# Transposed attention of a hybrid encoder step: three sets of head pages, gates in slices, values ahead of the last four query tiles, samples beside the last heads

## The chip, the cores and the metric

The kernel runs on one core of one Trainium2 chip. A core has TensorE (PE, the matmuls, with PEld for its weight loads), VectorE (DVE), ScalarE (ACT), GpSimd (POOL) and SyncE (SP, which here only issues DMAs). ACT and POOL issue DMAs as well. Each engine works through its own list of instructions in order. The metric is the device time of one execution in microseconds (us); lower is better.

## What is computed

One inference step of a two-layer encoder. 1168 frames pass through it: 16 meta tokens and 1024 prompt frames of one stream (1040 together, TP in the code) and 8 samples of 16 frames that continue running streams. Each layer has three groups of heads, and this case is about the first, latent attention with 8 heads:

```python
q = (rms_norm(c_q, q_norm) @ w_uq).reshape(B, L, MLA_HEADS, MLA_NOPE + MLA_ROPE)
q_nope, q_rope = q[..., :MLA_NOPE], apply_rope(q[..., MLA_NOPE:], pos)
...
k_nope = jnp.einsum('bkr,rhd->bkhd', c_kv, w_uk)
v = jnp.einsum('bkr,rhd->bkhd', c_kv, w_uv)
...
p = jax.nn.softmax(jnp.where(mask, sc.astype(jnp.float32) * scale, -jnp.inf), axis=-1)
o = jnp.einsum('bhlk,bkhd->blhd', p, v[:, :n_keys])
...
mixed = jnp.concatenate([o_a * jax.nn.silu(z_a), o_m * jax.nn.silu(z_m), o_g * jax.nn.silu(z_g)], axis=-1)
return x + mixed @ w_out, ...
```

The samples do the same attention over 1056 cached latent rows each, in the absorbed form (scores against the latent itself). The other two groups (mLSTM and gated DeltaNet) are through, but for the last of their gates, when the part that is changed begins.

## The kernel before

Data lie in pages, SBUF tiles of 128 partitions by 1200 numbers; there are 28. The program is written by generators ("threads": `gload`, `att_m`, `att`, `samp_load`, `samp_s`, ...) and one main thread (`projs`, then `qkv`, `out_first`, `out_proj`). A planner, `Weave`, runs them against a clock of its own that only matmuls and waits advance: a thread yields a number of us, or the name of something that must be done; when no thread is ready, the main thread gives its next few matmuls as filling. Thus the order of TensorE's matmuls is fixed when the program is built. The framework then places the other engines' instructions, so the lists of ACT and POOL can differ somewhat from the order in the source.

In each layer the attention goes like this. `qkv` makes six query tiles (j of 0 to 5; tiles 0 and 3 hold the rotary part, and two DVE operations and one of POOL a slice write it), stores them to DRAM (`qS`), loads four gated pages of the other groups with `mixload`, makes four key tiles (`kS`), and then the values in nine chunks into six pages (`VV`), among which it splits the four loaded pages into a high and a low part (`mixsplit`, 12 casts on ACT, L437, and 12 subtractions). `gload` loads the queries and keys of one head into a set of four pages and splits them (casts L1523 on ACT, subtractions L1524 on POOL); there are two sets, so head h's load waits until the scores of head h - 2 are all issued (`D1["hd", h - 2]`). `att_m` takes the row maxima of a head (17 or 18 score matmuls and as many reductions L1551), turns them with one transposition (L372), and sends the row through DRAM: ACT stores it (L1559), POOL loads it into partition 112 of `qh` (L383). Only then do the transposed scores of this head in `att` pass: 18 steps a head, in slices of 3, 6 and 9 key blocks; a step is three score matmuls (the first needs no row), an `Exp` on ACT (L1586) and, three steps behind (`LA`), a value product. At the end of a slice DVE takes a reciprocal (L1610) and a product, POOL multiplies by the gate (L1612). The gates of two heads lie in a page `za`, loaded by `gload`, stored by SP after the pair.

`out_first`, the first third of the output projection (96 groups of three matmuls), is the filling beside the heads. The samples follow: `samp_prep`, loads of the cache pages (`latT`, `latN`), `samp_split` (casts L1697 on ACT), scores `samp_s` and products `samp_t`, both of which wait for the end of the attention (`yield "att"`).

## Time and profile before

| | |
|---|---|
| median of 3 runs | 2755.3 us (2754.82 to 2755.98) |
| profiled execution: time | 2752.79 us |
| its span, first to last instruction | 2750.9 us |
| mean granted clock of TensorE | 0.962 |
| end of the projections to end of attention, layer 0 | 843.4 to 1181.9 us |
| the same, layer 1 | 2202.1 to 2536.3 us |

The profiled execution is one more run of the same program. The time of a run is some 2 us longer than the span of its instructions. A clock of 1.00 is TensorE's full speed, 0.50 half of it; a mean between them tells how much of a stretch ran at half speed. A line number names the line of the source; matmuls all stand at L361, in the helper `mm`, and are told apart by their tiles: `pb<-pg,pg` with 96 to 113 rows are scores, `pa<-wk,pg` value products, `pa<-pg,wh` projections.

### The profile page before, as it was taken

How to read it: one execution, taken by the hardware profiler on the slowest of the kernel's cores; microseconds unless marked ns; L12 is line 12 of the kernel's file. 1: busy time of each engine (PE TensorE's matmuls, PEld its weight loads, DVE VectorE, ACT ScalarE, POOL GpSimd, SP SyncE). 2: the span in 40 equal slices, each digit the busy share in tenths (PEclk: the TensorE clock that was granted, in tenths of full speed). 3: DMA queues.
4: the chain of work that ended last, by engine and by line, in shares of the span. 5: the costliest groups of instructions: out<-in, count | busy, mean ns of one | idle time of the engine just before them, and what ended most of it. 6: DMA issues, size and time to landing. Idle time of an engine off the chain costs nothing. (4 is left out here: it accounts for less than half of the span.)

```text
span 2750.9 us, 45261 instructions
## 1 busy us (share of the span) xinstructions
PE 2529.8 (92%) x17310; PEld 2176.9 (79%) x17310; DVE 1533.6 (56%) x3716; ACT 1120.6 (41%) x2635; POOL 753.8 (27%) x857
## 2 busy tenths in 40 slices
PE   6999999999998998789998999999999979987897
PEld 4787888878878886579977878787887878866897
DVE  6677375564352555455565764756544435555736
ACT  5454444544442333343343644444444333333612
POOL 3122222131132423232431231222211333322414
PEclk9999999999999998799999999999999999988898
DMA  3212121121126542264422122212211365312932
GB/s 132 64 41 72 50 71 59 58 67 56 49 88 183 148 118 60 82 193 172 151 79 51 49 65 61 68 49 68 65 49 47 108 184 145 105 51 82 309 114 85
DMA packets 152648, 257.57 MB, mean 94 GB/s; under 512 B 47296, under 2 KB 103216, under 8 KB 152432
## 3 DMA queue, kind: packets, MB, share of 16 engines
q1 hardware_dynamic: 150688, 251.82, 29.6%
q0 software_dynamic: 1472, 2.80, 0.5%
q8 instruction: 137, 2.24, 0.3%
q14 instruction: 79, 0.65, 0.1%
q10 hardware_dynamic: 272, 0.07, 0.0%
HBM read 189.70 MB, written 64.92 MB: 93 GB/s over the span
## 5 line engine op out<-in xcount | busy, mean ns | idle before, releaser
L361 PE MATMUL pa<-pg,wh 128*128 128x384 f32 (+2 forms) x6324 | 1313.6, 352 | 37.6 <-DVE wk L1425 8.4
L361 PEld LDWEIGHTS pa<-pg,wh 128*128 128x128 f32 x6324 | 1111.7, 191 | 76.0 <-DVE wk L1425 9.0
L361 PE MATMUL pb<-pg,pg 128*128 128x128 f32 (+23 forms) x1908 | 446.2, 354 | 62.4 <-DMA pg<-row 34.3
L361 PE MATMUL pa<-pg,wb 128*128 128x384 bf16 (+1 forms) x2208 | 421.4, 330 | 4.7 <-POOL pg L544 3.5
L361 PEld LDWEIGHTS pb<-pg,pg 128*128 128x128 f32 (+7 forms) x1908 | 313.1, 198 | 130.0 <-DMA pg<-row 38.7
L361 PEld LDWEIGHTS <-wb 128*128 128x128 bf16 x2208 | 201.8, 98 | 142.3 <-issue 30.2
L441 POOL TENSOR_TENSOR wh<-wf,wh 128x1024 fp32r<-128x1024 f32 (+1 forms) x61 | 144.5, 2368 | 347.2 <-ACT wh L437 346.8
L361 PE MATMUL pb<-wk,pg 128*128 128x128 f32 (+4 forms) x2168 | 219.9, 248 | 16.6 <-ACT wk L983 5.7
L1586 ACT ACTIVATE wk<-pb 128x320 f32<-128x320 f32 (+8 forms) x288 | 116.0, 407 | 276.9 <-PE pb L361 273.6
L361 PEld LDWEIGHTS pb<-wk,pg 128*128 128x128 f32 (+3 forms) x2168 | 191.2, 160 | 37.9 <-issue 16.5
L361 PE MATMUL pa<-wk,pg 128*128 128x320 f32 (+8 forms) x576 | 200.1, 438 | 1.3 <-DVE wk L1885 1.3
L437 ACT CAST wh<-wf 128x1024 fp32r<-128x1024 f32 (+1 forms) x122 | 126.4, 1036 | 137.9 <-PE pa L361 116.5
L1551 DVE TENSOR_REDUCE sm<-pb 128x1 f32<-128x348 f32 (+9 forms) x232 | 107.6, 491 | 106.5 <-PE pb L361 102.1
L1610 DVE RECIPROCAL wk<-pa 64x320 f32<-64x320 f32 (+2 forms) x48 | 110.6, 2305 | 80.4 <-PE pa L361 78.9
L361 PE MATMUL pb<-wk,wk 32*32 32x16 f32 (+6 forms) x1776 | 110.7, 216 | 15.1 <-DVE wk L1131 5.2
L441 DVE TENSOR_TENSOR wh<-wf,wh 128x1024 fp32r<-128x1024 f32 (+1 forms) x61 | 84.3, 1382 | 63.6 <-ACT wh L437 63.0
L868 DVE SCALAR_TENSOR_TENSOR pg<-pg,vec,pg 128x1192 f32<-128x1192 f32 x72 | 107.3, 1506 | 18.3 <-ACT pg L866 17.9
L1612 POOL TENSOR_TENSOR pg<-wk,pg 64x320 f32<-64x320 f32 (+2 forms) x48 | 43.9, 915 | 252.7 <-DVE pg L1611 244.9
L361 PEld LDWEIGHTS pa<-wk,pg 128*128 128x128 f32 (+1 forms) x576 | 105.2, 205 | 7.4 <-issue 1.4
L457 ACT CAST wb<-wf 128x1024 bf16<-128x1024 f32 x92 | 96.2, 1045 | 26.8 <-PE pa L361 20.1
L693 ACT COPY pg<-pa 128x384 f32<-128x384 f32 (+1 forms) x108 | 52.1, 482 | 132.0 <-PE pa L361 130.8
L361 PEld LDWEIGHTS pb<-wk,wk 32*32 32x32 f32 (+2 forms) x1776 | 73.2, 122 | 33.6 <-issue 9.5
(298 smaller groups left out, 3242.8 us busy)
## 6 DMA issues: line engine op xcount, KB each, us to landing
wf<-win SPq DMA_DIRECT2D x92, 512.0 KB
pg<-latT SPq DMA_DIRECT2D x32, 520.0 KB
pg<-latN SPq DMA_DIRECT2D x32, 512.0 KB
wf<-wout SPq DMA_DIRECT2D x24, 512.0 KB
xa<-wk SPq DMA_DIRECT2D x40, 192.0 KB
mix<-pg SPq DMA_DIRECT2D x12, 584.0 KB
pg<-mix SPq DMA_DIRECT2D x12, 584.0 KB
mix<-pg SPq DMA_DIRECT2D x12, 576.0 KB
```

Of the source, the lines that this page charges most:

```text
L361: W.last = P.matmul(out, lhsT, rhs, start=start, stop=stop)
L437: S.copy(hi, src)
L441: lo_eng.tensor_sub(lo, src, hi.bitcast(F32))
L457: S.copy(wb[:, :n], wf)
L693: S.copy(o[:, s0:s1], ps)
L868: V.scalar_tensor_tensor(y[:, :n], cb[:, j:j + n], vcol(l, "cw", 4 * ti + j), y[:, :n], op0=ALU.mult, op1=ALU.add)
L1551: V.tensor_reduce(mx[:LEN[c], 3 * c + i_:3 * c + i_ + 1], ps[:LEN[c], :n1 - x_], axis=AX.X, op=ALU.min)
L1586: S.activation(pt[:m, :b - a], ps, AF.Exp, scale=-1.0)
L1610: V.reciprocal(rc, po[d, :w])
L1612: G.tensor_mul(z, rc, z)
```

## The change

- Query tiles: only tiles 0 and 1 are made ahead of the keys; the values follow the keys, then the query tiles 2 to 5, then the loads of `mixload` and, after 8 us of the planner's clock, the splits of `mixsplit`. They used to stand among the values. A head's load waits for its query tile (`D1["qt", g]`).
- Head pages: three sets in place of two. Head h's load waits for head h - 3.
- Gates: no `za` pages. Each slice of a head loads its own gate (64 partitions by 320 to 384) into a small tile and stores it from ACT when POOL has multiplied: 24 loads on SP and 24 stores on ACT a layer in place of 4 and 4.
- `att` waits for the values at its first value product, not at its first score.
- Samples: `samp_s` and `samp_t` no longer wait for the end of the attention; `samp_t` takes PSUM tiles only when the attention's accumulator leaves one (`free_pa`).

TensorE's matmuls are the same in number and kind.

```diff
-            gr = 0
-            for j in range(6):
-                if j % 2 == 0:
-                    wh, wl = nxt
-                    nxt = load(j // 2 + 1 if j < 4 else "k")
+
+            def qtile(j, wh, wl):
+                gr = j - 1 - j // 3
                 while not room(1):
                     yield "idle"
...
-                    gr += 1
+                    D1["qt", gr] = 1
                 free(sg)
-            free(*cqh, *cql, *tab)
-            D1["qs"] = 1
-            while not room(2 * (PARTS[0][1] - PARTS[0][0])):
-                yield "idle"
-            A["mx0"] = mixload(*PARTS[0])
+
+            (wh, wl), nxt = nxt, load("k")
+            yield from qtile(0, wh, wl)
+            yield from qtile(1, wh, wl)
             for j in range(4):
                 if j == 0:
-                    wh, wl = nxt
-                    nxt = load("v")
+                    (wh, wl), nxt = nxt, load("v")
...
-            wh, wl = nxt
-            A["w0"] = load("o")
-            sp = mixsplit(A["mx0"])
+            (wh, wl), nxt = nxt, load(1)
...
-                next(sp, None)
-                next(sp, None)
                 yield
-            for _ in sp:
-                pass
             D1["v"] = 1
             free(*ckh, *ckl)
+            for j in (2, 3, 4, 5):
+                if j % 2 == 0:
+                    (wh, wl), nxt = nxt, load(2 if j == 2 else "o")
+                yield from qtile(j, wh, wl)
+            free(*cqh, *cql, *tab)
+            D1["qs"] = 1
+            A["w0"] = nxt
+            while not room(2 * (PARTS[0][1] - PARTS[0][0])):
+                yield "idle"
+            A["mx0"] = mixload(*PARTS[0])
+            t0 = W.t
+            while W.t < t0 + 8000.0:
+                yield "idle"
+            for _ in mixsplit(A["mx0"]):
+                yield "idle"
...
                 yield ("spill", g)
-                if h < 2:
+                yield ("qt", g)
+                if h < 3:
...
-                    yield ("hd", h - 2)
-                    qh, ql, kh, kl = sets[h % 2]
+                    yield ("hd", h - 3)
+                    qh, ql, kh, kl = sets[h % 3]
...
                 D1["grp", h] = W.t / 1000.0
-                if j == 0:
-                    yield from need(1)
-                    A["za", g] = pg()
-                    ld(A["za", g][:, o0:TP], mixS[8 + g][:, o0:TP])
-                    D1["za", g] = 1
...
-            yield "v"
...
+                    if j == 0:
+                        zt[h, s_] = z = wt("Og", 512)[64 * (h % 2):64 * (h % 2) + 64, :b - a]
+                        ld(z, mixS[8 + h // 2][64 * (h % 2):64 * (h % 2) + 64, a:b])
...
-                        if h > 5:
-                            free(*A["sets"][h % 2])
+                        if h > 4:
+                            free(*A["sets"][h % 3])
...
                     if j == 0:
+                        yield "v"
...
-                        if ("za", h // 2) not in D1:
-                            yield ("za", h // 2)
...
-                        rc, z = wt("hp", 528, 3)[r, :w], A["za", h // 2][r, q0:b]
+                        rc, z = wt("hp", 528, 3)[r, :w], zt.pop((h, s_))
                         V.reciprocal(rc, po[d, :w])
                         V.tensor_mul(z, po[r, :w], z)
                         G.tensor_mul(z, rc, z)
                         A["po"] = 0
-                        if s_ == 2 and h % 2:
-                            st(mixS[8 + h // 2][:, o0:TP], A["za", h // 2][:, o0:TP])
-                            free(A["za", h // 2])
+                        S.dma_start(mixS[8 + h // 2][r, q0:b], z)
...
         def samp_s():
-            yield "att"
             for b in range(8):
...
-                    yield 0.00
+                    if "att" in D1:
+                        yield 0.00
...
-                yield from need(1)
                 Pp = pg()
...
+        def free_pa():
+            while A.get("po", 0) and npa[0] - A["po"] > 1:
+                yield 0.2
+
         def samp_t():
-            yield "att"
             for b in range(8):
...
+                    yield from free_pa()
                     ps = pa()
```

What the planner makes of it is seen in three places. The first is TensorE's list at head 4 of layer 0. In the rows `pb<-cst,wk` at L372 is the transposition of the row maxima, `pa<-wk,pg` a value product, and 80x336, 128x256, ... are the score matmuls of a slice. Before:

```order
L361 MATMUL pa_10867<-wk_10916,pg_9499 128x64
L372 MATMUL pb_10937<-cst,wk_10812 128x128
L361 MATMUL pb_10952<-pg_9401,pg_9404 80x336
L361 MATMUL pb_10963<-pg_9584,pg_9582 128x348
L361 MATMUL pb_10966<-pg_9401,pg_9404 128x256
L361 MATMUL pb_10973<-pg_9584,pg_9582 128x348
L361 MATMUL pb_10976<-pg_9401,pg_9404 128x128
L361 MATMUL pb_10988<-pg_9584,pg_9582 128x344
L361 MATMUL pb_10991<-pg_9401,pg_9404 80x384
L361 MATMUL pb_10999<-pg_9584,pg_9582 128x456
L361 MATMUL pb_11002<-pg_9401,pg_9404 128x384
L361 MATMUL pb_10952<-pg_9401,pg_9403 80x336
```

The transposition of head 4's maxima stands between the last value product of head 3 (above it) and head 4's scores: the first of them on `pg_9404` need no row, those on `pg_9403` do, ten rows after the transposition. Now:

```order
L361 MATMUL pb_10646<-pg_9214,pg_9216 128x384
L361 MATMUL pb_10646<-pg_9215,pg_9216 128x384
L361 MATMUL pa_10623<-wk_10596,pg_9308 128x128
L372 MATMUL pb_10658<-cst,wk_10426 128x128
L361 MATMUL pa_10666<-pg_9678,wh_9914 128x384 x2
L361 MATMUL pa_10666<-pg_9679,wh_9914 128x384
L361 MATMUL pb_10674<-pg_9214,pg_9217 128x384
L361 MATMUL pb_10674<-pg_9214,pg_9216 128x384
L361 MATMUL pb_10674<-pg_9215,pg_9216 128x384
```

The same transposition stands amid the scores of head 3 (`pg_9214` to `pg_9217`) and the output projection (`wh_9914`); head 4's first score is the 87th row after it. It is like this for heads 2 to 7 of both layers.

The second place is the start of head 0 in layer 0, on TensorE. Before, the transposition of head 0's maxima, and the output projection behind it:

```order
L372 MATMUL pb_9797<-cst,wk_9594 128x128
L361 MATMUL pa_9810<-pg_9346,wh_9658 128x400 x2
L361 MATMUL pa_9810<-pg_9347,wh_9658 128x400
L361 MATMUL pa_9810<-pg_9348,wh_9658 128x400 x2
L361 MATMUL pa_9810<-pg_9349,wh_9658 128x400
```

Now, from the end of the last query tile (`wh_9445`) on:

```order
L361 MATMUL pa_9658<-pg_9055,wh_9445 128x384
L372 MATMUL pb_9670<-cst,wk_9385 128x128
L361 MATMUL pb_9695<-pg_9375,pg_9373 128x348
L361 MATMUL pb_9698<-pg_9375,pg_9373 128x348
L361 MATMUL pb_9701<-pg_9375,pg_9373 128x344
L361 MATMUL pb_9704<-pg_9375,pg_9373 128x456
L361 MATMUL pb_9709<-pg_9214,pg_9217 80x336
L361 MATMUL pb_9715<-pg_9375,pg_9373 128x456
L361 MATMUL pb_9718<-pg_9214,pg_9217 128x256
L361 MATMUL pb_9724<-pg_9375,pg_9373 128x392
L361 MATMUL pb_9727<-pg_9214,pg_9217 128x128
```

No output projection follows any more; behind the transposition stand row maxima of head 1 (`pg_9375,pg_9373`) and those scores of head 0 that need no row. The first that needs it is the 15th row.

The third place is ACT's list at the change from head 6 to head 7 in layer 0: L1589 is `Exp`, L1697 and L1700 are the casts of the samples' cache pages, and L1616 is the new store of a gate slice. Now:

```order
L1589 ACTIVATE wk_11715<-pb_11711 128x64
L1697 CAST pg_11705<-pg_11696 128x528 x2
L1589 ACTIVATE wk_11736<-pb_11732 80x336
L1589 ACTIVATE wk_11748<-pb_11744 128x256
L1589 ACTIVATE wk_11761<-pb_11757 128x128
L1697 CAST pg_11724<-pg_11699 128x528 x2
L1700 CAST pg_11739<-pg_11702 96x528 x2
L1697 CAST pg_11751<-pg_11718 128x528 x2
L1616 DMA mix<-wk_11580 64x320
L1589 ACTIVATE wk_11775<-pb_11771 80x384
```

Before, the casts of the first cache pages stood beside head 7 as well, but their loads were issued at head 6's start; now the loads are issued near head 6's end. The store L1616 stands one or two `Exp` after the point of the program where it was written.

## Rows read from the trace of the kernel before

**Rows 1.** The profile's page: span and the engines' busy us, share of the span, instructions.
```profile
span 2750.9 us, 45261 instructions
PE 2529.8 (92%) x17310; PEld 2176.9 (79%) x17310; DVE 1533.6 (56%) x3716; ACT 1120.6 (41%) x2635; POOL 753.8 (27%) x857
```

**Rows 2.** Windows, layer 0: length, busy us (count) per engine, clock, DMA share, GB/s.
```profile
843.00:899.00 56.00, 46.12 (x235) 43.82 (x234) 12.45 (x23) 17.98 (x37) 18.27 (x25) 0.91 0.73 212
899.00:937.00 38.00, 33.04 (x157) 29.09 (x156) 23.79 (x41) 11.82 (x26) 20.68 (x23) 0.91 0.55 154
937.00:1050.00 113.00, 110.24 (x594) 96.83 (x594) 66.03 (x97) 38.97 (x90) 32.53 (x35) 0.98 0.38 110
1050.00:1182.00 132.00, 103.91 (x452) 81.08 (x451) 62.30 (x98) 44.57 (x113) 32.47 (x42) 0.79 0.22 61
```

**Rows 3.** Windows, layer 1, the same stages, columns as above.
```profile
2202.00:2258.00 56.00, 44.23 (x224) 42.87 (x224) 10.99 (x20) 16.63 (x34) 16.55 (x21) 0.91 0.71 202
2258.00:2296.00 38.00, 31.32 (x151) 28.02 (x150) 24.29 (x39) 13.11 (x30) 22.45 (x26) 0.91 0.57 147
2357.00:2402.00 45.00, 41.50 (x209) 36.29 (x208) 22.93 (x34) 14.39 (x34) 13.62 (x15) 0.89 0.36 105
2402.00:2536.00 134.00, 110.58 (x517) 88.81 (x516) 72.36 (x109) 50.02 (x126) 38.67 (x49) 0.86 0.24 69
```

**Rows 4.** Waits of TensorE, layer 0, 1050 to 1182: us, times, longest.
```profile
PE pb L361 <- DMA pg<-row: 17.9, 4, 7.0
```

**Rows 5.** Waits of TensorE, layer 1, 2357 to 2536.
```profile
PE pb L361 <- DMA pg<-row: 16.3, 5, 5.1
```

**Rows 6.** Waits of TensorE, layer 0, 843 to 1050.
```profile
PE pa L361 <- ACT pg L1488: 4.5, 2, 2.4
PE pa L361 <- DVE wh L441: 3.8, 1, 3.8
```

**Rows 7.** Timeline of TensorE, heads 5 and 6: start, us, work [idle before, releaser].
```profile
1088.75 2.26 PE L361 MATMUL pb<-pg,pg 113*80 113x336 f32 x8 [4.21 <-DMA pg<-row]
...
1112.08 0.30 PE L372 MATMUL pb<-cst,wk 128*128 128x128 f32 x1 [2.55 <-DVE wk L1553]
...
1124.57 2.26 PE L361 MATMUL pb<-pg,pg 113*80 113x336 f32 x8 [7.00 <-DMA pg<-row]
```

**Rows 8.** Timeline of TensorE: value products of successive steps, head 0 and head 7.
```profile
948.04 0.81 PE L361 MATMUL pa<-wk,pg 128*128 128x384 f32 x2
...
951.49 0.81 PE L361 MATMUL pa<-wk,pg 128*128 128x384 f32 x2
...
1176.63 0.70 PE L361 MATMUL pa<-wk,pg 128*128 128x320 f32 x2
...
1177.62 0.70 PE L361 MATMUL pa<-wk,pg 128*128 128x320 f32 x2
```

**Rows 9.** All DMAs from or into the row of maxima (tile row).
```profile
DMA to landing us min/median/max: 1.7/2.5/5.9
```

**Rows 10.** Waits of GpSimd over the whole span.
```profile
POOL pg L383 <- DMA row<-wk: 29.8, 7, 8.9
```

**Rows 11.** Timeline of GpSimd at head 6's row.
```profile
1114.93 3.76 POOL L1524 TENSOR_TENSOR pg<-pg,pg 96x520 fp32r<-96x520 f32 x3
1118.63 0.55 POOL L383 DMA_DIRECT2D pg<-row  x1
```

**Rows 12.** Timelines of VectorE and GpSimd: a slice's normalising and gating.
```profile
1169.65 2.25 DVE L1610 RECIPROCAL wk<-pa 64x336 f32<-64x336 f32 x1 [8.27 <-PE pa L361]
1171.92 0.51 DVE L1611 TENSOR_TENSOR pg<-pa,pg 64x336 f32<-64x336 f32 x1
...
1172.57 0.90 POOL L1612 TENSOR_TENSOR pg<-wk,pg 64x336 f32<-64x336 f32 x1 [6.54 <-DVE pg L1611]
```

**Rows 13.** ScalarE: casts of mixsplit (count, ns), and a cast of a cache page.
```profile
L437 ACT CAST pg<-pg x12: 514/527/532, 896.2 to 909.7; 128x384 fp32r<-128x384 f32 x8, 128x400 fp32r<-128x400 f32 x4
...
1203.16 1.17 ACT L1697 CAST pg<-pg 128x528 fp32r<-128x528 f32 x2 [7.51 <-DMA pg<-latT]
```

More of the change, by code (lines that the diff above doesn't have):

```diff
@@ L1535, in att_m @@
                 yield ("grp", h)
-                qh, ql, kh, kl = A["sets"][h % 2]
+                qh, ql, kh, kl = A["sets"][h % 3]
                 mx = sm(32, "mx", bufs=2)
@@ L1567, in att @@
             steps = [(h, s_, j) for h in range(8) for s_ in range(3) for j in range(9) if QB[j] < QS_[s_][1]]
-            fly, po = [], None
-            yield "v"
+            fly, po, zt = [], None, {}
             for i_ in range(len(steps) + LA):
@@ L1577, in att @@
                     a, b = max(QS_[s_][0], QB[j]), QS_[s_][1]
+                    if j == 0:
+                        zt[h, s_] = z = wt("Og", 512)[64 * (h % 2):64 * (h % 2) + 64, :b - a]
+                        ld(z, mixS[8 + h // 2][64 * (h % 2):64 * (h % 2) + 64, a:b])
                     m = 80 if j == 0 else 128
-                    qh, ql, kh, kl = A["sets"][h % 2]
+                    qh, ql, kh, kl = A["sets"][h % 3]
                     ks = slice(KB[j], KB[j] + m)
@@ L1775, in samp_t @@
                     yield 1.70
+                yield from free_pa()
                 ps = pa()
@@ L1787, in samp_t @@
                     mm(po[:, q_:q_ + 128], lnp[r][:, 1024:1152], pte, False, True)
-                    yield 0.00
+                    if "att" in D1:
+                        yield 0.00
                 for r in range(2):
```

## The prediction

> **What bounds the kernel now.** I read the page first: TensorE is busy for 2529.8 of 2750.9 us [rows 1], and no other engine for much over half. The change leaves the matmuls as they are, so the time can move only by TensorE's idle time, and by the time that it runs at half clock. The windows by stage are the second view. In layer 0 the middle heads, beside the output projection, have 110.24 busy us in 113 at a clock of 0.98; the last heads, where that filling is used up, have 103.91 in 132 at 0.79 [rows 2]. Layer 1 is the same: 0.89 and 0.86 in the last two windows [rows 3]. The reader is to see two losses in one place there: idle time, and a clock that falls beside it. The third view says what ends the idle time: the row of maxima, for 17.9 us in 4 waits in layer 0 [rows 4] and 16.3 us in 5 in layer 1 [rows 5]. The fourth, the timeline, shows one such wait: transposition at 1112.08 (after 2.55 us of waiting), then the matmuls that need no row, then 7.00 us of nothing until the score at 1124.57 [rows 7].
>
> **What is removed: the waits at the last heads.** The order shows head 4's transposition ten rows ahead of the first score that needs the row; now it is 87 rows ahead. A row of matmuls on that stretch takes some 0.5 us (12.2 us from the end of the transposition to that score, less 7.00 of waiting, over ten rows), so the row has some 40 us where the path took 12. These waits go.
> Layer 0: idle 132 - 103.9 = 28.1 us. A clock of 0.79 is a mean of 1.00 and 0.50, so 42% of 132 = 55 us passed at half speed. If all the idle time lay in it, 27 busy us ran at half speed and would have taken 14 less; if none did, 28 less. I take 21.
> Layer 1, last two windows: idle 3.5 + 23.4 = 26.9; half speed 22% of 45 + 28% of 134 = 47 us, so 10 to 24 lost; I take 17.
> Together 28 + 21 + 27 + 17 = 93 us. The stages won't be perfect; I put back what the filled stage loses (2.8 us idle, and 4% of 113 at half speed, 2 us): 5.5 a layer, **11**. Bounds of this term: a gain of 70 (the low clock losses and twice the rest put back) to 93.
>
> **Among the projections.** Keys waited 3.8 us for their split weights, and values 4.5 us for copies on ACT [rows 6], which shares its time there with the 12 casts of `mixsplit` (0.53 us each, [rows 13]). The casts move out, and the key weights are now asked for before query tile 0; but the third set of query weights now stands at the same distance, two tiles, as the key weights did. Half of both, 4 us, and half as much again for the clock (0.91 there): 6 a layer, **12** in all (0 to 20).
>
> **What is added: head 0.** Before, 96 groups of output projection lay behind head 0's transposition; now 14 rows lie there, some 7 us at 0.5. The path from transposition to row needed 12.2 us at head 6, where POOL began its row load at 1118.63, behind 3.76 us of subtractions for a head load [rows 11]. It has the same neighbours at head 0 (subtractions for heads 1 and 2), and more: the loads of `mixload` are issued just ahead of it. A row's DMA lands after 1.7 us at best, 2.5 usually, 5.9 at worst [rows 9]. So idle time of 4.2 (head 5's wait, [rows 7]) to 2.55 + 7.00 + 3.4 = 13 us; I take 8, near head 6, and half as much again for clock: between 0.75 us per idle us of the late stage (21 / 28) and next to nothing in the projections. 12 a layer, **24** in all (bounds 8 to 40). The cover here was free before; with it gone, this is the price.
> A rule of the Trainium skill bears on this, in "Trainium Kernel Development and Optimization", section "Key Constraints": DMAs issued by SP, ACT and POOL run on the same 16 DMA engines and interleave. That speaks against putting big loads next to the row; by it the row here lands nearer 5.9 than 2.5, 3 us worse a layer.
>
> **Smaller edits.** The 12 casts of `mixsplit`, 6.3 us of ACT, now stand among head 0's `Exp`s, which otherwise take no more than a third of ACT (38.97 busy us in 113, [rows 2]). `Exp` runs three steps ahead of its product, and a step is 1.7 us with filling (two steps from 948.04 to 951.49), 0.99 us bare [rows 8]: a lead of 3 to 5 us absorbs a few casts, not all. 2 a layer, **4** (0 to 12).
> Samples, layer 0: the cache pages' loads were issued at the start of head 6 and now near its end (the third set of head pages holds the room). ACT's casts on them stand in the same place, so ACT can stand still, with head 7's `Exp`s behind them, and TensorE three steps later. After the attention ACT was seen to wait 7.51 us for such a load [rows 13]. Less the lead of 3 us, and some clock: **7** (0 to 12), layer 0 alone. The `latN` half of these loads also comes later, for the first products: **3** (0 to 9). The scores of the first samples that now stand beside head 7 fill nothing that isn't already counted.
> Head loads one head earlier and 24 gate loads on SP instead of 4: SP has nothing behind them but loads for later heads, and the DMA engines are a quarter to a third busy [rows 2, 3]; nothing, with 3 us against it if I am wrong.
>
> **The gate stores on ACT.** There are 48 in all, and each waits for a chain: reciprocal 2.25, product 0.51, POOL 0.90, from 1169.65 to 1173.47, 3.8 us [rows 12]. What stands behind the store on ACT is `Exp`, and behind that TensorE. The order has the store one or two `Exp` later than written, 1 to 3.4 us by [rows 8], which leaves 0.4 to 2.8 us of standing still, against a lead of three steps, 3 us. I take nothing. The upper bound: 2.8 - 1 = 1.8 us each, 48 x 1.8 = 86.
>
> **Sum.** -93 + 11 - 12 + 24 + 4 + 7 + 3 = -56. The profiled execution took 2752.79, so 2696.8; the median lies 2.5 above it: 2699. I say **2698**.
>
> **Rivals.**
> Slower: ACT held by the gate stores. The place is the end of each slice, the price up to 1.8 us for each of 48, against a gain of 56: from 1.2 us a store on there is no gain, and at 1.8 the time is 2755 - 56 + 86 = 2785. For it: an engine that issues a DMA does wait here, POOL stood 29.8 us in 7 waits for the row's landing [rows 10], and POOL may be late for its multiplication by a subtraction of 1.25 us (3.76 for three, [rows 11]). Against it: TensorE is three steps ahead, and only a slice of three key blocks (one in three) has the next slice's end close.
> The Trainium skill speaks for this rival in "DMA: Bandwidth & Descriptors", "Anatomy of one DMA — SWDGE (gpsimd) path": a DMA engine doesn't wait on semaphores, the wait is on the engine that issues it, ahead of dispatch. POOL's waits agree. By that sentence each store costs ACT the whole rest of the chain; what it costs TensorE, the page doesn't say.
> Smaller gain: the row path stays late, since POOL loads it between the subtractions of the head loads, and three sets now crowd these. Half of the waits at the last heads would stay: 93 / 2 = 46 less, 2745. Against it: the 40 us of lead are three times the path of 12.
> No change: head 0 at its upper bound (16 more), late samples at theirs (11 more), `mixsplit` too (8), and a smaller gain at the late heads (12) eat 47 of the 56. That is mishaps together, so unlikely.
> Better: head 0's wait is hidden by row maxima of head 1 (16 less), and the projections gain their 20: 2698 - 24 = 2674, and with neither sample term 2664.
>
> **How the numbers follow.** The forecast with its terms inside their bounds has 0.75; better than 2664, 0.06; a gain of 8 to 20 us, 0.07; no change, 0.04; slower, 0.08. A measurement of this kernel tells some 0.2% (5.5 us) from no change. Faster is 0.75 + 0.06 + 0.07 = 0.88. The range goes from 2664 (all favourable bounds) to 2732 (the forecast, with head 0 and the samples at their upper bounds, 27, and a further 7 of `mixsplit`), which leaves out some 2 in 10.
>
> **What would show it.** Right: windows of the last heads at a clock of 0.93 or more with idle time under 5%; waits for the row only at head 0 (4 to 13 us a layer); no wait of keys on `wh`; from the end of the projections to the end of the attention some 338.5 - 28 - 21 + 5.5 - 6 + 12 + 2 + 7 = 310 us in layer 0, plus what of the samples now lies inside; ACT waiting for `latT` at head 7 of layer 0, not of layer 1. Wrong: TensorE's waits at the heads name `Exp` (now L1589) and ACT's wait ahead of it names POOL's gating (now L1614); or the row is still waited for at heads 4 to 7; or a clock under 0.9 without idle time, which the sum has no term for.

## The result and the profile after

The changed kernel takes 2648.7 us (median of 4 runs, 2645.9 to 2655.1), the kernel before 2755.6: a ratio of 0.9615 (95% interval 0.9598 to 0.9633), 106 us faster. The forecast was 2698 with a range that ended at 2664, so the direction was right and the size was half of what came. The profiled execution is the longest of the four (2655.1); 6 us of that lie ahead of the changed part, which begins, with the first query tile's matmuls, at 842.1 and not at 835.8 us as before. (The table before the change counts from 843.4, 7.6 us into that tile's matmuls.) From the end of a layer's projections to the next layer's first matmul (in layer 1 to the end), layer 0 went from 551.0 to 499.4 us and layer 1 from 556.3 to 504.0: 104 us, half in each.

By the page, TensorE is now busy for 2494.3 us of a span of 2653.3 (94%); it was 2529.8 of 2750.9 [rows 1].

The windows by stage, which answer to [rows 2, 3]; columns as there. The stages are: end of the projections to the transposition of head 0's maxima; head 0, to head 1's transposition; heads 1 to 7, to the last `Exp`; and the rest of the layer.

```profile
842.00:907.00 65.00, 59.98 (x319) 56.22 (x318) 25.88 (x50) 25.82 (x53) 38.12 (x45) 0.97 0.66 178
907.00:928.00 21.00, 18.14 (x71) 13.48 (x70) 9.00 (x17) 6.09 (x15) 3.58 (x6) 0.76 0.67 196
928.00:1136.00 208.00, 202.71 (x1102) 176.79 (x1101) 138.13 (x202) 83.14 (x208) 73.07 (x84) 0.99 0.42 120
1136.00:1341.00 205.00, 184.94 (x1161) 178.03 (x1159) 110.26 (x191) 73.67 (x166) 71.58 (x79) 0.94 0.50 173
...
2149.00:2213.00 64.00, 58.66 (x313) 55.22 (x311) 26.64 (x50) 25.30 (x52) 36.74 (x44) 0.97 0.66 177
2213.00:2231.00 18.00, 16.61 (x69) 12.99 (x68) 8.73 (x16) 5.70 (x13) 4.91 (x8) 0.81 0.74 230
2231.00:2439.00 208.00, 202.99 (x1083) 175.97 (x1082) 130.00 (x187) 80.02 (x200) 68.96 (x79) 0.97 0.41 115
2439.00:2653.00 214.00, 188.87 (x1184) 178.78 (x1182) 126.51 (x227) 73.95 (x171) 72.19 (x87) 0.93 0.49 164
```

Two things are to be read there. The heads are full: 202.7 busy us of 208 at a clock of 0.99 in layer 0. And the first stage, 93 and 96 us long before, takes 65 and 64, with 5 us of idle time in each. Some 19 of these 28 and 32 us are busy time (78.7 and 78.1 us before, 60.0 and 58.7 now), for the most part work that now stands later (390 and 387 matmuls before, 319 and 313 now); the rest is idle time. The same stages of both kernels, idle us and clock from this view; "loss" is an estimate of what half speed took from busy time, worked out as in the prediction (the middle between half the half-speed time, and half of what of it is not idle):

| stage | layer 0 before | after | layer 1 before | after | change of idle + loss | forecast |
|---|---|---|---|---|---|---|
| to head 0's transposition | 14.3, 0.91 | 5.0, 0.97 | 18.4, 0.91 | 5.3, 0.97 | -13 - 17 = **-30** | -12 |
| head 0 | 1.0, 1.00 | 2.9, 0.76 | 1.0, 1.00 | 1.4, 0.81 | +6.1 + 3.4 = **+10** | +24 |
| heads 1 to 7 | 30.3, 0.87 | 5.3, 0.99 | 27.8, 0.89 | 5.0, 0.97 | -45 - 35 = **-80** | -93 + 11 = -82 |
| rest of the layer | 17.3, 0.96 | 20.1, 0.94 | 26.1, 0.92 | 25.1, 0.93 | +6 - 3 = **+3** | +4 + 7 + 3 = +14 |

These sum to -97, and the lengths say -104; the 7 between them is what the estimate of the loss leaves open. In the last column the 14 are the smaller edits together. The forecast expected 4 of them (`mixsplit`) and 7 (samples) beside the heads, so only the 3 for `latN` belong to the last row for certain.

TensorE's waits in layer 0, up to the last `Exp` and, behind the dots, from there to the next layer (us, times, longest); they answer to [rows 4, 6]:

```profile
PE pa L361 <- DVE wk L1423: 4.4, 1, 4.4
PE pb L361 <- DMA pg<-row: 1.1, 1, 1.1
...
PE pa L372 <- ACT pg L1752: 7.1, 3, 4.1
PE pb L361 <- DMA pg<-latN: 3.7, 1, 3.7
```

The row of maxima is waited for once, for 1.1 us, at head 0, where 17.9 us stood in the last heads alone. Keys on `wh` are gone from the list, and values wait 0.3 us for their copies (now L1482). The 7.1 us for the `Exp` of the samples (L1752) are not new: before, the same `Exp` (then L1753) was waited for 5.2 and 1.9 us there. New are the 3.7 us for the cache page `latN`.

### The profile page after: what moved, and what is told of

It reads as the page before. It is cut to its first block, busy times and chain, and to the rows that moved or that the text cites. A ratio compares the mean times of both kernels' runs of the same rounds, so it can differ in the third digit from the quotient of the medians.

```text
span 2653.3 us, 45522 instructions
## 1 busy us (share of the span) xinstructions
PE 2494.3 (94%) x17310; PEld 2154.2 (81%) x17310; DVE 1529.8 (58%) x3716; ACT 1115.5 (42%) x2635; POOL 763.2 (29%) x865
## 5 line engine op out<-in xcount | busy, mean ns | idle before, releaser
L361 PE MATMUL pa<-pg,wh 128*128 128x384 f32 (+3 forms) x6324 | 1320.5, 352 | 25.5 <-DVE wk L1423 8.8
L361 PE MATMUL pb<-pg,pg 128*128 128x352 f32 (+26 forms) x1908 | 427.4, 339 | 17.7 <-DVE sm L1552 4.4
L361 PEld LDWEIGHTS pb<-pg,pg 128*128 128x128 f32 (+7 forms) x1908 | 302.5, 189 | 71.1 <-issue 14.9
L441 POOL TENSOR_TENSOR wh<-wf,wh 128x1024 fp32r<-128x1024 f32 (+1 forms) x61 | 144.1, 2363 | 325.1 <-ACT wh L437 318.7
L361 PEld LDWEIGHTS pb<-wk,pg 128*128 128x128 f32 (+3 forms) x2168 | 195.2, 162 | 43.0 <-issue 16.8
L1589 ACT ACTIVATE wk<-pb 128x320 f32<-128x320 f32 (+8 forms) x288 | 113.9, 406 | 244.9 <-PE pb L361 221.4
L361 PE MATMUL pa<-wk,pg 128*128 128x320 f32 (+8 forms) x576 | 192.5, 420 | 1.8 <-ACT wk L1589 1.3
L1530 POOL TENSOR_TENSOR pg<-pg,pg 64x520 fp32r<-64x520 f32 (+1 forms) x64 | 87.0, 1370 | 104.8 <-ACT pg L1529 91.1
L441 DVE TENSOR_TENSOR wh<-wf,wh 128x1024 fp32r<-128x1024 f32 (+1 forms) x61 | 78.9, 1293 | 47.3 <-ACT wh L437 47.0
L361 PEld LDWEIGHTS pa<-wk,pg 128*128 128x128 f32 (+1 forms) x576 | 98.8, 195 | 5.9 <-ACT wk L1589 1.8
```

Of the source, the lines that this page charges most:

```text
L361: W.last = P.matmul(out, lhsT, rhs, start=start, stop=stop)
L441: lo_eng.tensor_sub(lo, src, hi.bitcast(F32))
L1530: G.tensor_sub(lo, raw, hi.bitcast(F32))
L1589: S.activation(pt[:m, :b - a], ps, AF.Exp, scale=-1.0)
```

## Experiments

Three theories went into the first ones. **A**: the stages add up, so each edit is worth what its stage shows. **P**: the prediction's terms. **F**: the new order only shifts filling (the output projection) to the late heads. The runs below are given as ratios to the kernel before, with their intervals; 0.001 is 2.75 us.

| run | what | ratio | interval | us against before, by the ratio |
|---|---|---|---|---|
| e12 | changed kernel again | 0.9631 | 0.9617 to 0.9645 | -102 |
| e1 | two sets | 0.9891 | 0.9872 to 0.9910 | -30 |
| e2 | old order | 0.9738 | 0.9721 to 0.9755 | -72 |
| e3 | new order alone | 0.9885 | 0.9868 to 0.9902 | -32 |
| e5 | three sets alone | 0.9764 | 0.9748 to 0.9780 | -65 |
| e6 | gate pages again | 0.9896 | 0.9879 to 0.9913 | -29 |
| e11 | gate pages, thread of their own | 0.9709 | 0.9696 to 0.9722 | -80 |
| e4 | gate stores on SP | 0.9659 | 0.9637 to 0.9681 | -94 |
| e7 | samples wait | 0.9587 | 0.9571 to 0.9602 | -114 |
| e8 | tile 1 before tile 0 | 0.9611 | 0.9594 to 0.9627 | -107 |
| e9 | old order, key weights early | 0.9721 | 0.9708 to 0.9734 | -77 |
| e10 | old order, mixsplit behind the values | 0.9730 | 0.9712 to 0.9748 | -74 |
| e13 | old order, both, mixload late | 0.9732 | 0.9719 to 0.9745 | -74 |
| e14 | e7, sample queries spread | 0.9573 | 0.9559 to 0.9588 | -118 |
| e15 | ten short waits | 0.9666 | 0.9653 to 0.9680 | -92 |

**e12** is the changed kernel once more, beside e9 to e11.

> The changed kernel once more, beside the others on one chip. Both theories: ratio 0.9615 within 0.002, and waits and clock as in the first trace; it gives e9 to e11 a neighbour of their own.

It agrees with the first measurement within the intervals.

### The third set and the order

**e1**, two sets in the changed kernel:

```diff
-                if h < 3:
+                if h < 2:
...
-                    yield ("hd", h - 3)
+                    yield ("hd", h - 2)
```

> The changed kernel with two sets of head pages again (a head's load waits for head h - 2); the new order of query tiles and values, the gate slices and the samples stay. Theory A (stage by stage): the third set alone removed the row waits and the half clock at the last heads, 82 us of the 107, so this one takes about 2648.7 + 82 = 2731. Theory F (filling): much of that came from the new order, since the output projection that used to lie behind head 0's row is now left over for the last heads; then this kernel loses only about half, 2690. Waits for the row: by A some 25 to 35 us again in both layers, by F under 17.

76 us are lost, as A has it. The row is waited for again, 20.1 us in 11 waits, less than the 25 that were expected; the rest stands under other names, and in the clock, 0.86 and 0.88 over heads 4 to 7 by the windows. F is out as the main cause.

**e2**, the old order of `qkv` in the changed kernel (the lines of the change's diff in `qkv`, taken back):

```diff
-            yield from qtile(0, wh, wl)
-            yield from qtile(1, wh, wl)
+            for j in range(6):
+                if j % 2 == 0:
+                    (wh, wl), nxt = nxt, load(j // 2 + 1 if j < 4 else "k")
+                yield from qtile(j, wh, wl)
```

> The changed kernel with the old order of qkv (six query tiles, mixload, keys, values with mixsplit among them); three sets, gate slices and samples stay. Theory A: the old order loses 29 us among the projections (weights of the keys, copies of the values, clock) and gives back 10 at head 0, so 2648.7 + 19 = 2668. Theory P, the terms of the prediction: the old order is better by the 24 of head 0 and the 4 of mixsplit, less 12 among the projections, so 2648.7 - 16 = 2633. Waits by A: keys on wh 3 to 4 us and values on their copies 4 to 5 us a layer are back; head 0's row waits are gone in both.

The old order is 34 us slower, so P is wrong even in sign: what it counted as a cost of 16 is a gain. **e3** is the new order alone, in the kernel before: `qkv` as in the change's diff, and

```diff
                 yield ("spill", g)
+                yield ("qt", g)
```

> The kernel before with the new order of qkv alone; two sets, gate pages and waiting samples stay. Theory A: 2755.6 - 19 = 2737. Theory P: 2755.6 + 16 = 2772. Theory F: the filling saved at head 0 moves to heads 3 to 5 and takes away some of their waits, so another 20 to 40 lower than A, about 2705; the waits for the row at the last heads fall from 34 us to under 20.

32 us faster, nearly the 34 of e2. The row waits fell from 34.3 to 25.2 us in both layers, so F has a small part here. **e5** is the third set alone:

```diff
-                if h < 2:
+                if h < 3:
...
-                    yield ("hd", h - 2)
+                    yield ("hd", h - 3)
```

> The kernel before with three sets of head pages alone: old order of query tiles and values, gate pages, samples waiting. Theory A (parts add up): the third set is worth the 72 to 76 us that separate the kernels with and without it so far, so a ratio of about 0.973 to before (2755 to 2681). Theory R (room): the gate slices made the room for the third set, and without them the four pages come late, so the row waits of the last heads stay in part: ratio 0.985 to 1.0. By A the waits for the row in layers 0 and 1 together are under 3 us, by R over 10.

65 us, between A and R, nearer A. Its row waits, 6.3 us in 3, lie between the two as well. So the order is worth 32 to 34 and the set 65 to 76, and 32 + 65 = 97 is most of the 106. (The samples take some 8 back, e7 below, so that about 17 come from the parts together.)

### What the gate slices are for

**e6** puts the gate pages back:

```diff
-                        S.dma_start(mixS[8 + h // 2][r, q0:b], z)
+                        if s_ == 2 and h % 2:
+                            st(mixS[8 + h // 2][:, o0:TP], A["za", h // 2][:, o0:TP])
+                            free(A["za", h // 2])
...
+                if j == 0:
+                    yield from need(1)
+                    A["za", g] = pg()
```

> The changed kernel with the gate pages of the kernel before (one page for two heads, loaded by the head loads, stored by SP after the pair) in place of the slices. Theory A: the slices change nothing by themselves, ratio to before 0.9615 within 0.002. Theory R: they make room; with the pages back the sample pages or the third set come later, 10 to 30 us slower, ratio 0.965 to 0.972. Rival S in a small way (ACT held by its gate stores): a few us faster, ratio under 0.960.

77 us of the 106 are gone; this was outside all three expectations. SP's timeline shows the key loads of heads 2, 3 and 4 in layer 0 of e6:

```profile
910.95 0.48 SPq L383 DMA_DIRECT2D pg<-kS  x1
982.44 1.04 SPq L383 DMA_DIRECT2D pg<-kS  x1
993.85 0.45 SPq L383 DMA_DIRECT2D pg<-kS  x1
...
```

and those of the changed kernel:

```profile
894.82 0.55 SPq L383 DMA_DIRECT2D pg<-kS  x1
934.20 0.45 SPq L383 DMA_DIRECT2D pg<-kS  x1
968.37 0.45 SPq L383 DMA_DIRECT2D pg<-kS  x1
```

A head's load every 30 to 40 us in the one; in the other head 3's stands 72 us behind head 2's and head 4's 11 behind that. In the code the load of the odd head stands behind `need(1)` for its pair's gate page. **e11** tests just that: a thread of its own loads the gate pages.

```diff
+        def zload():
+            for g in range(4):
+                yield ("grp", 2 * g)
+                yield from need(1)
+                A["za", g] = pg()
```

> As e6 (gate pages, three sets, new order), but a thread of its own loads the gate pages, so that a head's load doesn't stand behind the wait for a gate page. In e6 heads 3, 5 and 7 were loaded 50 to 70 us behind the head ahead of them, and 11 us ahead of the next. Theory H: the gate page held the head load, and that is the whole loss; head loads come every 30 us again, and the ratio is 0.962 to 0.966. Theory R: 28 pages are too few for gate pages, three sets and the early values in any order; something else waits (the attention for its gate, the output projection's pages), ratio 0.975 or more.

51 of the 77 us come back: the head load that stood behind the gate page was two thirds of it. Head loads come every 30 to 40 us again. The other third fits R: in layer 1, TensorE waits 8.0 us for `mixsplit`'s subtraction, in e11 as in e6, which the changed kernel doesn't show. That this is the whole of the third is not shown. The slices were priced at nothing. No run has them alone; e1, which has them and the early samples, is as fast as e3 without either, so by themselves they earn little more than those samples cost. But in the new order, with the gate pages loaded as before, the third set shows no gain (e6, with the early samples, is as fast as e3).

**e4**, the stores of the slices on SP:

```diff
-                        S.dma_start(mixS[8 + h // 2][r, q0:b], z)
+                        st(mixS[8 + h // 2][r, q0:b], z)
```

> The changed kernel with the 48 stores of the gate slices issued by SP, not by ACT; nothing else changes. ACT stood up to 4.3 us for one of them in the trace. Theory A: TensorE's lead of three steps covers that, so 2648.7 within 3 us. The slower rival's mechanism at work in a small way: 5 to 15 us faster, 2634 to 2644. If SP's queue delays head loads behind a store that waits, slower, up to 20 us.

Not faster; 8 us slower by the ratio than e12, whose interval overlaps, and 12 slower than the first measurement, whose interval nearly meets this one. What stood behind the stores on ACT in the changed kernel, whole span (us, times, longest):

```profile
ACT wk L1589 <- POOL wk L1614: 6.2, 2, 4.3
ACT pg L1529 <- POOL wk L1614: 4.2, 4, 1.6
ACT wk L1783 <- POOL wk L1614: 2.9, 1, 2.9
```

13 us in 7 waits for 48 stores, 0.3 us a store where the rival put up to 1.8. In e4 these rows are gone, and SP has, in layer 0 alone,

```profile
SPq L386 <- POOL wk L1614: 66.0, 17, 8.3
```

with the loads of the samples' pages among what queues behind: TensorE's wait for `latN` is 6.3 us, 3.7 before. So nothing speaks for moving the stores off ACT, and the slower rival's price was a sixth of its bound, under TensorE's lead.

### Among the projections

In e2 the waits of [rows 6] are back. Three runs take their suspects away one after the other. **e9** issues the key weights' load ahead of tile 3's stores:

```diff
+                if j == 3:
+                    nk = load("k")
```

> The changed kernel with the old order of qkv, as e2, but the load of the key weights is issued ahead of query tile 3, so that on SP it stands ahead of tile 3's eight stores and not behind them. In e2's trace SP issued it at 872.11, right behind those stores, which wait for tile 3's rotary work; TensorE then waited 3.8 us a layer for the split weights. Theory Q (queue): the distance in tiles doesn't matter, the place behind the stores does; the wait goes, with the clock 8 to 12 us less than e2 in both layers, ratio to before 0.9695 to 0.971. Theory D (distance, as the prediction had it): the load is bound by the free weight buffer and by its landing, and the wait stays at 2 us or more, ratio 0.973 to 0.975.

5 us better than e2, with intervals that overlap, and Q's reason is wrong. SP, ACT and TensorE in layer 0:

```profile
860.54 0.73 SPq L453 DMA_DIRECT2D wf<-wuk  x1
...
873.58 1.04 ACT L437 CAST wh<-wf 128x1024 fp32r<-128x1024 f32 x1
...
888.46 1.04 ACT L437 CAST wh<-wf 128x1024 fp32r<-128x1024 f32 x1 [6.06 <-DMA wf<-wuv]
...
875.93 8.84 PE L361 MATMUL pa<-pg,wh 128*128 128x348 f32 x54 [2.77 <-DVE wh L441]
889.91 5.46 PE L361 MATMUL pa<-pg,wh 128*128 128x348 f32 x18 [5.13 <-ACT pg L1466]
```

The load is issued 12 us earlier (860.54, not 872.11), but ACT casts the weights at 873.58, right behind its last copy of query tile 5 and with no wait for a DMA ahead of it; 2.77 us of waiting stay. The cast of the next weights, the values', waits 6.06 us for its DMA, to 888.46, and the key copies behind that cast on ACT are waited for 5.13 us, where e2 waits 3.02. In layer 1 the wait for the key weights falls from 3.9 to 2.8 us as well, and that for the copies stays (2.4 and 2.6). No run moved the cast itself. **e10** moves `mixsplit`'s casts behind the values:

```diff
-                next(sp, None)
-                next(sp, None)
                 yield
...
             free(*ckh, *ckl)
+            for _ in sp:
+                yield "idle"
```

> The changed kernel with the old order of qkv, as e2, but mixsplit's 12 casts stand behind the nine value chunks and not among them. The prediction put half of the values' 4.5 us a layer (5.0 and 5.8 in e2) down to these casts. Theory M: all of it is theirs; the waits of values on their copies fall under 1 us a layer, and if head 0's cover is not late, ratio 0.968 to 0.971. The prediction's half: 2.5 us a layer stay, ratio 0.971 to 0.974. Rival: the casts come too late for the output projection behind head 0's transposition, a row wait of 4 us or more appears there, same as e2 or slower, 0.974 to 0.980.

TensorE's waits, layer 0, projections and head 0:

```profile
PE pa L361 <- DVE pg L441: 5.5, 1, 5.5
PE pb L361 <- DVE sm L1546: 3.1, 2, 2.9
PE pa L361 <- ACT pg L1490: 0.3, 1, 0.3
```

The values' wait on their copies fell from 5.0 to 0.3 us: all of it was the casts', not half. But the time is that of e2, since the output projection now waits 5.5 us for the split data, and row maxima 3.1. **e13** does both, and moves `mixload` behind the values too:

```diff
-            A["mx0"] = mixload(*PARTS[0])
             for j in range(4):
...
             free(*ckh, *ckl)
+            A["mx0"] = mixload(*PARTS[0])
+            t0 = W.t
+            while W.t < t0 + 8000.0:
+                yield "idle"
+            for _ in mixsplit(A["mx0"]):
+                yield "idle"
```

> The changed kernel with the old order of tiles, keys and values (six query tiles first), but the loads of mixload and the casts of mixsplit stand behind the values, as in the changed kernel, and the key weights are asked for ahead of tile 3. Theory M3: these three together are the gain among the projections, so idle time and clock loss there fall from 22 us a layer (e2) to 6 to 10; head 0 then has no cover and costs 5 to 7 as in the changed kernel; ratio 0.960 to 0.967. Theory O: the order itself (keys and values early, so that head 0 is loaded earlier) is the gain, and most of the 22 us stay; ratio 0.970 or more.

Windows: the first stage and head 0, layer 0, then layer 1:

```profile
838.00:913.00 75.00, 65.39 (x322) 59.97 (x321) 25.54 (x51) 25.14 (x51) 31.44 (x38) 0.92 0.67 191
913.00:948.00 35.00, 25.83 (x107) 21.64 (x107) 23.37 (x27) 12.17 (x28) 16.02 (x20) 0.68 0.40 95
2160.00:2232.00 72.00, 62.81 (x321) 57.20 (x320) 24.98 (x49) 25.07 (x51) 32.68 (x39) 0.96 0.70 201
2232.00:2265.00 33.00, 23.19 (x90) 19.03 (x90) 23.39 (x25) 11.47 (x27) 15.24 (x19) 0.63 0.34 76
```

The first stage has 9.6 and 9.2 us of idle time where e2 has 19.2 and 16.8; with the clock that is 13 and 11, a little over M3's 6 to 10. But head 0 now has 9.2 and 9.8 at clocks of 0.68 and 0.63, for the most part waits for row maxima (L1550, 5.7 and 7.7), not for the row, and the time is e2's. This is what was overlooked: in the new order the query tiles 2 to 5 stand between the values and head 0, and TensorE works on them while head 0 is loaded, split and searched for its maxima. With the old order that cover is the output projection, which needs `mixload` and `mixsplit` among the projections; take them out, and head 0 lies bare.

**e8** makes tile 1 ahead of tile 0, against the 4.4 us that are left (L1423):

```diff
-                    D1["qt", gr] = 1
+                    if j != 1:
+                        D1["qt", gr] = 1
...
+            yield from qtile(1, wh, wl)
             yield from qtile(0, wh, wl)
-            yield from qtile(1, wh, wl)
+            D1["qt", 0] = 1
```

> The changed kernel with query tile 1 made ahead of tile 0. TensorE's last long wait among the projections, 4.4 us a layer for the rotary operations of tile 0 on VectorE, stands at the start of the query tiles. Theory A: tile 0 waits for its tables there, which have landed a tile later; the wait goes, with the clock 5 to 6 us a layer, 2649 to 2638 (ratio 0.957). Rival: the rotary tile is the slow one wherever it stands, and behind it the head's load comes later: the wait moves to the keys or to head 0, same or up to 8 us slower.

No gain, as the rival said. TensorE, then ACT, layer 0, at the end of the keys:

```profile
868.28 8.38 PE L361 MATMUL pa<-wh,pg 128*128 128x512 f32 x24 [3.81 <-ACT pg L1460]
...
867.26 0.62 ACT L1531 CAST pg<-pg 96x520 fp32r<-96x520 f32 x1 [5.59 <-DMA pg<-qS]
```

The L1423 wait is down to 0.3 us, but ACT now stands 5.59 us at a cast of head 0's queries, whose store comes a tile later, with key copies queued behind it, and TensorE waits 3.81.

### Samples and the clock

**e7** lets the samples wait again:

```diff
         def samp_s():
+            yield "att"
...
         def samp_t():
+            yield "att"
```

> The changed kernel in which the samples' scores and products wait for the end of the attention again. Theory A: the early samples move work of TensorE only, and the time is the same within 5 us. Theory C (clock): in layer 1 one wait of 2.55 us for a sample's split beside head 7 was followed by some 14 us at half clock; with the samples behind the heads that wait goes, 6 to 9 us faster. The prediction's term (late samples of layer 0, 7 + 3): it is paid in head 7 by ACT, so held samples would take it out again, up to 10 us faster.

8 us faster than the changed kernel (0.9587 against 0.9615, with intervals that just meet; 12 us against e12), all in layer 0: 486.5 against 499.4 us for the layer's part, 504.4 against 504.0 in layer 1. The 46 us behind the heads of layer 0, the changed kernel first:

```profile
1136.00:1182.00 46.00, 32.11 (x188) 29.24 (x187) 25.67 (x39) 20.43 (x52) 15.09 (x24) 0.78 0.63 208
```

and e7:

```profile
1134.00:1180.00 46.00, 43.24 (x315) 40.96 (x314) 32.18 (x54) 27.62 (x73) 20.79 (x37) 1.00 0.90 280
```

13.9 us idle at a clock of 0.78, against 2.8 at 1.00. The wait that theory C names did not go: its 2.55 us stand in e7's layer 1 too, and layer 1 gained nothing. Nor is it the prediction's mechanism: ACT's waits in the changed kernel from 907 to 1137 have no `latT`, and the idle time lies behind head 7 and not in it. It is TensorE's waits behind the heads, for the samples' own `Exp` and for `latN`. That the first samples' scores, already made, leave less to fill these with is argued, not shown. **e14** adds 1.6 us between the groups of matmuls that make the sample queries:

```diff
                           bhl(ql[r])[:, :, h, :], V)
-                yield 0.00
+                yield 1.60
```

> e7 (samples wait for the attention) with 1.6 us between the eight groups of matmuls that prepare the sample queries, which ran one after the other and filled the PSUM tiles that the scores of head 7 need. In layer 1 TensorE waited 2.55 us for them and then ran 13 us at half clock. Theory L (lump): the wait costs its length and the half clock behind it, 2.5 + 6 = 8 to 9 us; e7's ratio 0.9587 falls to about 0.956. Theory I (idle time alone): 2.5 us, ratio 0.958. Rival: spread groups reach into the end of head 7, and the samples start later, same or slower.

By the ratios it can't be told from e7 (0.9573 and 0.9587), but the stage tells. TensorE of e7 in layer 1, with the windows around the wait and the whole of heads 4 to 7:

```profile
2399.35 6.37 PE L361 MATMUL pb<-pg,pg 96*128 96x320 f32 x21 [2.55 <-DVE pg L441]
...
2399.00:2404.00 5.00, 4.65 (x16) 3.66 (x17) 2.72 (x11) 2.27 (x9) 1.53 (x5) 0.59 0.79 251
2404.00:2409.00 5.00, 5.00 (x18) 3.85 (x16) 0.88 (x4) 1.79 (x6) 0.19 (x1) 0.50 0.36 104
2409.00:2414.00 5.00, 5.00 (x19) 3.90 (x17) 1.33 (x2) 1.88 (x5) 0.00 (x0) 0.55 0.00 1
2414.00:2419.00 5.00, 5.00 (x30) 4.40 (x29) 4.24 (x3) 3.29 (x8) 1.63 (x2) 1.00 0.00 0
...
2295.00:2428.00 133.00, 130.45 (x685) 111.97 (x683) 78.28 (x111) 50.33 (x127) 39.92 (x48) 0.95 0.40 118
```

The same heads in e14:

```profile
2295.00:2420.00 125.00, 124.95 (x684) 107.77 (x684) 78.21 (x111) 49.18 (x125) 37.56 (x47) 1.00 0.40 118
```

The wait of 2.55 us ended at 2399.35, and the windows from there to 2414 ran at 0.50 to 0.59. Without it these heads are 8 us shorter, 2.5 less idle time and 5.5 less busy time for the same matmuls. That is theory L's size, from one profiled execution of each. e14 has the lowest ratio here.

**e15** puts ten small matmuls in that should wait for an `Exp`:

```diff
+                    if s_ == 2 and j == 4 and 1 < h < 7:
+                        pd = pb()[:64, :64]
+                        mm(pd, pt[:m, :64], pt[:m, :64], True, True)
```

> The changed kernel with one more small matmul (64 columns) in the third slice of heads 2 to 6 of both layers, ten in all, that multiplies the last Exp's result with itself and so waits for that Exp in the middle of the stage whose clock is 1.00; its result is used by nothing. A wait of 0.4 to 0.8 us each. Theory L: even such waits drop the clock, 3 to 6 us each, 30 to 60 us in all (ratio 0.972 to 0.983). Theory I: 0.5 to 1 us each, 5 to 10 us (ratio 0.963 to 0.966), and the clock of these heads stays at 0.98 or more.

Eight of the ten found their `Exp` done, with a gap of 0.05 us or less ahead of them. Two waited, one in each layer:

```profile
1110.31 0.68 PE L361 MATMUL pb<-pg,pg 96*128 96x320 f32 x3 [0.61 <-DVE pg L441]
1111.58 0.33 PE L361 MATMUL pb<-wk 128*64 128x64 f32 x2 [0.59 <-ACT wk L1589]
...
1109.00:1115.00 6.00, 4.81 (x18) 3.34 (x18) 3.25 (x13) 2.49 (x9) 1.54 (x5) 0.75 0.60 189
1115.00:1121.00 6.00, 6.00 (x19) 4.45 (x19) 1.36 (x5) 2.11 (x8) 0.00 (x0) 0.50 0.06 14
...
2389.82 0.33 PE L361 MATMUL pb<-wk 128*64 128x64 f32 x2 [0.33 <-ACT wk L1589]
```

Behind the first, 0.59 us, which follows on a wait of 0.61, the clock is 0.50 from 1112 to 1122: some 5 us lost (an estimate, half of these 10). e12 has the wait of 0.61 at the same place (L441) without the other, and its clock stays at 1.00. Behind the second, 0.33 us alone, the clock stays at 1.00. The ten matmuls' 3 us (0.33 each), 0.9 of waiting and these 5 make up the 10 us of difference to e12. So theory L's price came for one wait of the two, theory I's for the other, and with eight that did not wait the time can't tell them apart.

## Why the prediction fell short

**The late heads: right.** -82 forecast, -80 in the table; e1 and e5 put 65 to 76 us on the third set. The wait for the row is at head 0 alone, as was said. The lead is shorter than the 40 us that were worked out from 87 rows: from the end of the transposition to the first score that needs the row it is 13 to 24 us at heads 2 to 7 of layer 0, which is still more than the path. The lower bound of this gain doesn't follow either: 79 less twice the 11 is 57, not 70. What was not seen is on what the gain rests: the slices were argued to cost nothing, and what they give was not asked: room, and head loads that stand behind no gate page (e6, e11).

**Among the projections: the failed step is "half of both, 4 us".** The two waits went all but 0.3 and 0.6 us, and with them the copies of the keys (L1462, 5.3 us in both layers), which had no term: 22 us of idle time less, where 8 were counted. The reason for halving the keys' wait was the distance of two tiles; e9 shows that it isn't the distance, and not the place on SP either, but, by e9's rows, the cast's place in ACT's list. The values' wait was all the casts' (e10). One wait taken out alone came back under another name in layer 0 (e9, e10); the new order takes out the chain.

**Head 0: "I take 8, near head 6" was mis-sized**, +24 for +10. From the end of the transposition the path took 7.9 us, not 12.2: in the changed kernel's timeline (TensorE, then GpSimd)

```profile
907.23 0.27 PE L372 MATMUL pb<-cst,wk 128*128 128x128 f32 x1
...
912.38 0.64 PE L361 MATMUL pb<-pg,pg 112*128 112x328 f32 x1 [0.59 <-DVE sm L1552]
913.62 0.69 PE L361 MATMUL pb<-pg,pg 96*128 96x384 f32 x1 [0.59 <-DVE sm L1552]
915.37 2.26 PE L361 MATMUL pb<-pg,pg 113*80 113x336 f32 x8 [1.06 <-DMA pg<-row]
...
905.84 1.30 POOL L1530 TENSOR_TENSOR pg<-pg,pg 96x520 fp32r<-96x520 f32 x1
...
911.73 0.53 POOL L383 DMA_DIRECT2D pg<-row  x1 [0.30 <-issue]
```

the transposition is at 907.23 and the first score that needs the row at 915.37. GpSimd's subtractions for the next head had ended by 907.14, so its row load was issued 4.2 us behind the transposition's end, 6.3 at head 6; what stood ahead of it was a subtraction of output weights, which ended at 911.43. The 12.2 us were also the longest of their kind: in the kernel before, the other seven heads of layer 0 took 6.1 to 8.3. And the cover was misjudged: "the cover here was free before; with it gone, this is the price" holds in e13, where head 0 costs 18 to 20 us a layer by the same estimate, more than the 12 forecast. In the changed kernel query tiles 2 to 5 are the new cover, which the term left out. The rule of the Trainium skill that DMAs of all queues share 16 engines ("Trainium Kernel Development and Optimization", "Key Constraints") was to make the row late by 3 us a layer. At head 0 the row load took 3.6 us in both layers, from issue to landing, against 2.1 in the median of all; in layer 0 the DMA engines were 1.00 and 0.90 busy from 912 to 918. Before, it took 2.6 and 3.7 us there, so at most layer 0's row was late by the rule, by 1 us. TensorE waited 1.1 and 0.8 us for it, so the rule did not decide.

**Smaller edits.** Forecast +14, the table +3 in its last row. For the samples the size was right and the mechanism wrong: 10 were forecast, 7 of them for ACT's wait for `latT` ahead of head 7's `Exp`, and e7 measures 8 by the ratios and 13 by the stage (10 against e12); but ACT had no such wait, and the loss lies behind the heads. That the 10 met it is luck; the 3 for `latN` met 3.7. That the last row rose by only 6 in layer 0 means that something else gained some 7 there; which edit, stays open. No run has the edit to `yield "v"` alone. The casts of `mixsplit` run in one block on ACT, from 932.8 to 937.9, and no `Exp` is waited for there. What they cost came through VectorE, which does a part of the subtractions (L441): TensorE waited 0.5 and 1.1 us for it, until 936.7 and 939.0, with 3 us at half clock behind, and 1.3 and 0.5 us at the same place in layer 1. That is some 5 us by estimate, for 4 forecast, and lies in the rows of the heads.

**The gate stores: right.** ACT stood 13 us for them, and TensorE's waits for an `Exp` come to 1.3 us in layer 0, at head 7, and none in layer 1. The rule of the Trainium skill that a wait stands on the engine that issues the DMA ("DMA: Bandwidth & Descriptors", "Anatomy of one DMA — SWDGE (gpsimd) path") agrees with e4: the waits moved to SP with the stores. What stands there cost little on ACT and more on SP.

Together: -18 (projections), -14 (head 0), -11 (smaller) and +2 (late heads) are 41 of the 50 us by which the forecast was short; 7 more lie between the table and the lengths. The rival that came nearest is "better", with head 0 hidden and the projections' 20 gained; it had a chance of 0.06, and the gain went 15 us beyond its 2664. From the end of the projections to the end of the attention, as the prediction counts it, layer 0 took 287.8 us (849.6 to 1137.4) where it said 310.

## What to carry to other kernels

Price a moved block by what it now stands beside, not only by what it left: the query tiles that moved behind the values were head 0's new cover. Waits that stand in one chain (load, cast, copy, next load) went only together here; taking out one of them showed little. An edit that is priced at nothing can carry most of another's gain: ask for every page or buffer what waits for it, and what stands behind that wait.

## What the runs showed of the hardware

A short wait in a busy stage can cost more in clock than in idle time. In e14's pair 2.5 us of idle time came with 5.5 us of slower matmuls; in e15 waits of 0.61 and 0.59 us, close together, came with some 5. At head 0 of the changed kernel, in windows of 3 us,

```profile
909.00:912.00 3.00, 2.19 (x6) 0.89 (x5) 2.42 (x6) 0.00 (x0) 2.62 (x2) 0.99 0.55 148
912.00:915.00 3.00, 1.33 (x2) 0.57 (x2) 0.83 (x2) 0.00 (x0) 0.26 (x1) 0.50 1.00 226
915.00:918.00 3.00, 2.63 (x10) 2.31 (x11) 0.00 (x0) 1.36 (x4) 0.00 (x0) 0.50 0.90 297
918.00:921.00 3.00, 3.00 (x10) 2.60 (x9) 0.43 (x1) 0.64 (x2) 0.00 (x0) 0.50 1.02 409
```

the clock is 0.50 from 912 to 921, and stays there for two windows after TensorE is busy again, for waits of 0.2 to 1.1 us. It isn't always so: in e15 0.33 us alone, and in e12 0.61 us alone, left the clock at 1.00; and the first stage of layer 0, with a wait of 4.4 us (L1423), ran at 0.97 over its 65 us, which is a loss of 2 us at most. The forecast took a fixed share of the idle time, 0.5 to 0.75, for the clock; it was 1.5 times the idle time at head 0 (4.3 for 2.9, by estimate), 2.2 times in e14's pair, and under half in that first stage. No fixed share fits these places.
